# Order of the DMA transposes between two token blocks of a hybrid decoder block, with its low-rank products and router moved

## The chip, the core and the metric

The kernel runs on one core of a Trainium2 chip. The core has TensorE for matmuls, VectorE, ScalarE and GpSimd (POOL) for the rest, and SyncE, which here does nothing but hand DMAs to one queue in program order. All engines run at the same time and wait for each other through semaphores. The metric is the time of the device for one call, in microseconds (us), as the median of several runs.

## The reference

One decoder layer over 2048 tokens of width 1024. It computes a gated linear attention (GLA) and a multi-scale causal pooling from the same normed input, gates and merges the two, projects the result, and feeds it to a mixture of experts (32 experts in 4 groups, the best group and its two best experts for each token).

```python
h = rmsnorm(x, norm1_g)
q, k, v, r, a_low, u_pool, gate_gla, gate_pool = jnp.split(h @ w_in, split_idx, axis=-1)
log_a = jax.nn.log_sigmoid(a_low @ w_alpha_up + b_alpha) / 16.0      # a_low has 16 columns
o = gla_mix(q, k, v, log_a)
o = head_rmsnorm(o, gla_norm_g) * jax.nn.silu(r)
merged = jax.nn.sigmoid(gate_gla) * (o @ w_gla_branch) + jax.nn.sigmoid(gate_pool) * (pool_mix(u_pool, ...) @ w_pool_branch)
x = x + merged @ w_out
h2 = rmsnorm(x, norm2_g)
x = x + hier_moe(h2, w_router_group, ..., w_exp_gate, w_exp_up, w_exp_down)   # router: 36 logits per token
return rmsnorm(x, norm_f_g)
```

## The kernel before

The mixer, everything up to `h2` and the router, works through the tokens in four blocks of 512 (0 to 3), each as four tiles of 128 rows (t0 to t3). The experts follow when all blocks are done. Float32 values are split into a high and a low half of 16 bits, so a product of 128x128 by 128x512 is made of three matmuls ("passes"); in every block TensorE runs, one after another: `p3` (v and r, seven products of 24 matmuls each), `qk`, the GLA steps with the pooling's products between them, `gates(0)` and `merge(0)`, `gates(1)` and `merge(1)`, and the output product.

Operands with the contraction in the partitions come from transposes that the DMA engines make, issued on SyncE's queue (`TQ` is "sync"):

- `turned` (line 771) transposes one tile's half of GLA's or the merged rows. `merge(1)` makes four of them, one a tile, after `L845` on VectorE, `L847` on POOL, `L769` on ScalarE and `L770` on POOL. The output product `out_mm` (line 859) reads them as `mT[t][1]`; those of `merge(0)` are `mT[t][0]`.
- `p0_turn` (line 259) transposes the normed input of the next block: eight DMAs for tiles 0 and 2 (i = 0) and eight for tiles 1 and 3 (i = 1), of each eight four into `hT` and four into `hS` (sums of tiles, which `p3` and others use).
- `out_turn` (also line 259, `bt<-bt`) transposes the normed output rows `h2`, two DMAs a tile, for the router's logits (`logits`, line 881).

At the end of a block, `out_mm(t, 0)` and `out_mm(t, 1)` give the left and right half of tile t's output; the string `OUT` sets the order in which they and the work between them are written: `m0` and `n0` are the two halves of tile 0, `t0` is its `out_turn`, `b` is `p1b` and `c` is `p1c`. `p1a` (line 441) computes the 16 columns of `a_low` for the next block from all of `hT`: 24 narrow matmuls, four side by side, and one copy. `p1b` (line 453) expands them to 256 columns and takes the log-sigmoid and running sums on ScalarE (lines 458 to 463) and VectorE (466 to 468); `p1c` makes the decay factors. `out_norm` adds to x (line 862, VectorE), stores, and norms the row (lines 240, 242, 251).

A block's logits and its counting of tokens by expert (`route`, lines 1036 to 1128) are run inside the next block's `p3`: its list `fill` has one entry ahead of each product, `N2` empty ones, then the logits of t0 to t3; `route` follows `p3`.

What is written is not yet the order that runs. A scheduler with a cost model of its own orders each engine's instructions by what it expects to be ready; `issue_after(ins)` adds an edge, so that what is traced inside it and runs on the engine of `ins` stands behind `ins`. Each engine, SyncE's queue too, then runs its list strictly in order.

Where block b hands over to b + 1 is called boundary b here: the output product of b, with the transposes of b + 1, and the start of `p3` of b + 1. There are three, and block 0 differs in one point: the weights are loaded in float32 (line 159), split by ScalarE (175) and VectorE (176) and stored for later blocks (179), which load the halves (168).

Of the kernel before, what the change touches and what calls it, by code (L numbers as in the profile page):

```python
# [36 lines left out]
class Mixer:  # L37
# [727 lines left out]
    def turned(self, x, lo):  # L765

        nc = self.nc
        hl, o = self.bt([128, 2, 512], F16), self.bt([128, 8, 128], F16)
        nc.scalar.activation(hl[:, 0], x, AF.Copy)  # L769
        self.on(lo).tensor_tensor(hl[:, 1], x, hl[:, 0], op=OP.subtract)  # L770
        getattr(nc, self.TQ).dma_start(o, hl.rearrange("p a c -> p (a c)"), transpose=True)
        return o

    def pool_u(self, b, g):
# [47 lines left out]
        self.seven(self.L7, GG0 + 4 * c, GP0 + 4 * c, self.et, post, fill)  # L822
        return s

    N0, N1, N2, NK = 3, 0, 2, 3
    OUT = 'm0 m1 b m2 m3 w n0 c n1 t0 n2 t1 n3 t2 t3'
    LAST = 'm0 s0 m1 t0 s1 l0 f0 m2 t1 s3 l1 f1 n3 s4 l2 f3 r01 t3 l3 r23 f4'

    def merge(self, c, s, fill=()):
# [57 lines left out]
    def block(self, b, tail):  # L887

        last = b + 1 == self.NB
        self.blk = b  # L890
        self.hT, self.L7, self.L7c = self.hTn, self.sevens(self.Hn, self.HSn), self.sevens_c(self.Hn, self.HSn)
        self.kend = [None, None]
        self.oT, self.mixT, self.mT, self.xo = [], [None] * 4, [[] for _ in range(TT)], {}
        self.v, self.rs = {}, {}
        if b:
            self.p3([lambda: None] * self.N2 + tail[:4])
            tail[4]()
        else:
            self.p3([lambda: None] * 2 + [self.p1a, self.p1b, self.p1c])
        s0, s1 = self.qk(0), self.qk(1)  # L900
        for f in s0 + s1[:self.NK]:
            f()
        self.p2t(0)
        for f in s1[self.NK:]:
            f()
        self.p2t(1)
        steps = []
        for t in range(TT):
            g = self.gla_a(t)
            if t % 2 == 0:  # L910
                steps = self.pool_u(b, t)
            for f in steps[:4]:
                f()
            steps = steps[4:]
            self.gla_b(t, *g)
        sg = self.gates(0)
        self.merge(0, sg)
        nx, non = [], lambda: None
        steps = [] if last else self.p0_norm(b + 1, 0, nx)
        sg = self.gates(1, [non] * self.N0 + steps)  # L920
        if not last:
            self.p0_turn(0, nx, self.DM[1])
            nx = []
            steps = self.p0_norm(b + 1, 1, nx)
        self.merge(1, sg, [non] * self.N1 + steps)
        if not last:
            self.p0_turn(1, nx, self.DM[1])
            self.p1a()
        hh, h2 = {}, {}

        def turn(t):
            h2[t] = self.out_turn(hh[t], self.DM[2] and not (last and t >= self.DM[3]))

        def logits(t):
            self.logits(t, h2[t])

        def mm(t, hf, mid=None):
            self.out_mm(b, t, hf, wo, mid)
            if hf:
                hh[t] = self.out_norm(b, t, last and t >= self.QT)  # L940

        wo = {hf: [self.weight("wv", O0 + 4 * hf + j) for j in range(4)] for hf in range(2 if last else 1)}
        if last:
            nc = self.nc
            nc.vector.tensor_scalar(self.g2, self.g2, float(D) ** 0.5, None, op0=OP.mult)
            self.xo = {t: self.x_load(b, t) for t in range(TT)}
            mm(0, 0)
            self.early.close()
            self.mw = self.ctx.enter_context(self.tc.tile_pool(name="mw", bufs=1))
            s, n = self.weights(0), self.weights(1)  # L950
            for i in (0, 1, 3, 4):
                self.fetch(s, i)
            self.first = [s, n]

            def split(i):
                with self.tc.issue_after(self.done[-2]), self.tc.issue_after(self.done[-1]):
                    self.split1(s, i)

            def fetch(i):
                with self.tc.issue_after(self.turning):  # L960
                    self.fetch(n, i)

            acts = {"m": lambda t: (mm(t, 0), mm(t, 1)) if t else mm(t, 1), "t": turn, "l": logits,
                    "n": lambda t: (mm(t, 0), mm(t, 1, lambda: turn(t - 1))),
                    "s": split, "f": fetch}
            for c in self.LAST.split():
                if c[0] == "r":
                    self.route(b, int(c[1]), len(c) - 1)
                else:
                    acts[c[0]](int(c[1]))  # L970
            self.mid.close()
            self.mq = self.ctx.enter_context(self.tc.tile_pool(name="mq", bufs=1))
            self.gf = self.mq.tile([128, D], F32, name="gfr")
            self.nc.sync.dma_start(self.gf, self.A["gfr"].to_broadcast([128, D]))
            for i in (2, 5):
                self.fetch(s, i)
            return None
        def wo1():
            wo[1] = [self.weight("wv", O0 + 4 + j) for j in range(4)]

        acts = {"m": lambda t: mm(t, 0), "n": lambda t: mm(t, 1), "t": turn, "w": lambda t: wo1(), "b": lambda t: self.p1b(),
                "c": lambda t: self.p1c()}
        for c in self.OUT.split():
            acts[c[0]](int(c[1:] or 0))
        return [lambda t=t: logits(t) for t in range(TT)] + [lambda: self.route(b)]
# [673 lines left out]
```

## Time and profile before

| | us |
|---|---|
| median of 3 runs | 1665.48 |
| lowest, highest | 1657.59, 1665.78 |
| the profiled execution | 1663.56 |
| its span in the trace | 1661.7 |
| TensorE busy (matmuls) | 1517.5 |
| VectorE busy | 1064.5 |
| ScalarE busy | 650.6 |
| POOL busy | 519.9 |
| TensorE waiting for transposes of line 771 (L859) | 13.0 |
| TensorE waiting for transposes of line 259 into bt (L881) | 15.0 |
| mean granted clock of TensorE | 0.965 |

The boundaries lie at about 281 to 400 us (0), 545 to 660 (1) and 812 to 930 (2). An engine's idle time costs something only where TensorE, or what TensorE waits for, comes later by it.

### The profile page before, as it was taken

The page shows a single profiled execution, that of the slowest core. Times are in us where ns is not written, and L with a number is a line of the kernel's source. Part 1 is how long each engine was busy: PE and PEld are TensorE (multiplying, and loading weights), DVE is VectorE, ACT ScalarE, POOL GpSimd, SP SyncE. Part 2 cuts the span into 40 slices and gives each one's busy share as a digit, 9 for nine tenths or more (in the row PEclk, how much of TensorE's full clock was granted, in tenths as well). Part 3 has the DMA queues.
Part 4 walks back from the last instruction along what each step waited for, and adds up shares of the span by engine and source line. Part 5 has one row for each costly group of instructions (what it writes and reads, how often), then busy time and mean ns, then how long its engine had stood idle before and what let it go on. Part 6 is the DMA issues. An engine that isn't in the chain of part 4 may idle for free. (4 is left out here: it accounts for less than half of the span.)

```text
span 1661.7 us, 27589 instructions
## 1 busy us (share of the span) xinstructions
PE 1517.5 (91%) x10635; PEld 915.8 (55%) x10635; DVE 1064.5 (64%) x1941; ACT 650.6 (39%) x1023; POOL 519.9 (31%) x499
## 2 busy tenths in 40 slices
PE   4888997898999898999988999996799999999995
PEld 2365442345744344854433774443668687777873
DVE  8999796447744344772624774337577777777773
ACT  5633454431123241122323121123356665666651
POOL 1034243222414311432411341131333444444431
PEclk9899999999999999999999999998799999999998
DMA  8866678898466959566879755759599999999950
GB/s 289 253 226 213 215 258 186 275 367 247 153 194 198 255 167 293 173 198 179 212 198 255 235 169 177 215 155 313 193 320 331 333 329 341 334 328 327 321 190 36
DMA packets 247337, 400.96 MB, mean 241 GB/s; under 512 B 154731, under 2 KB 159211, under 8 KB 247200
## 3 DMA queue, kind: packets, MB, share of 16 engines
q1 hardware_dynamic: 224672, 330.79, 64.0%
q0 software_dynamic: 22528, 68.35, 11.6%
q8 instruction: 85, 1.39, 0.3%
q14 instruction: 52, 0.43, 0.1%
HBM read 300.33 MB, written 75.50 MB: 226 GB/s over the span
## 5 line engine op out<-in xcount | busy, mean ns | idle before, releaser
L1391 PE MATMUL acc<-xT,mwh 128*128 128x184 f16 (+2 forms) x3264 | 249.3, 238 | 0.0
L1391 PEld LDWEIGHTS <-mwh 128*128 128x128 f16 x3264 | 244.1, 98 | 7.7 <-issue 7.5
L859 PE MATMUL acc<-w,bt 128*128 128x512 f16 x768 | 173.1, 387 | 21.2 <-DMA bt<-bt 13.0
L842 PE MATMUL acc<-w,bt 128*128 128x512 f16 x768 | 170.0, 383 | 8.3 <-ACT w L175 8.3
L1297 DVE SCALAR_TENSOR_TENSOR mwh<-mst,mwh 128x1024 f16<-128x1024 f32 x128 | 153.4, 1219 | 24.0 <-ACT mwh L1296 24.0
L1296 ACT ACTIVATE mwh<-mst 128x1024 f16<-128x1024 f32 x128 | 128.8, 1049 | 54.1 <-PE acc L1391 53.3
L522 PEld LDWEIGHTS <-w 128*128 128x128 f16 x1344 | 129.5, 99 | 35.1 <-issue 11.6
L859 PEld LDWEIGHTS <-bt 128*128 128x128 f16 x768 | 75.7, 99 | 117.5 <-DMA bt<-bt 14.0
L842 PEld LDWEIGHTS <-bt 128*128 128x128 f16 x768 | 75.4, 98 | 101.5 <-issue 12.9
L339 PEld LDWEIGHTS <-hS 128*128 128x128 f16 x768 | 75.6, 98 | 95.0 <-issue 5.7
L175 ACT ACTIVATE w<-w 128x1024 f16<-128x1024 f32 x74 | 74.9, 1029 | 113.2 <-DVE w L398 33.5
L176 DVE SCALAR_TENSOR_TENSOR w<-w 128x1024 f16<-128x1024 f32 x74 | 98.3, 1342 | 29.9 <-ACT w L175 29.6
L1416 PE MATMUL acc<-msd,sg 128*128 128x512 f32 x256 | 115.7, 604 | 0.0
L847 POOL TENSOR_TENSOR et<-et 128x512 f32<-128x512 f32 x32 | 43.4, 1358 | 201.6 <-DVE et L845 201.6
L522 PE MATMUL acc<-hS,w 128*128 128x256 f16 x768 | 93.4, 274 | 4.7 <-DVE w L176 3.0
L339 PEld LDWEIGHTS <-hT 128*128 128x128 f16 x576 | 56.3, 98 | 71.4 <-issue 5.1
L769 ACT ACTIVATE bt<-et 128x512 f16<-128x512 f32 x48 | 30.1, 628 | 167.1 <-POOL et L847 105.6
L845 DVE SCALAR_TENSOR_TENSOR et<-acc,et 128x512 f32<-128x512 f32 x64 | 43.5, 689 | 80.4 <-PE acc L842 80.4
L339 PE MATMUL aux<-w,hS 128*128 128x512 f16 x384 | 89.7, 384 | 3.0 <-DVE et L757 2.6
L339 PE MATMUL acc<-w,hS 128*128 128x512 f16 x384 | 88.3, 379 | 0.0
L819 ACT ACTIVATE et<-et 128x512 f32<-128x512 f32 x64 | 39.6, 628 | 101.8 <-DVE et L348 101.7
L1416 PEld LDWEIGHTS acc<-msd,sg 128*128 128x128 f32 x256 | 47.8, 192 | 55.8 <-issue 46.7
(307 smaller groups left out, 2602.1 us busy)
## 6 DMA issues: line engine op xcount, KB each, us to landing
w<-wkeep SPq DMA_DIRECT2D x210, 512.0 KB, 4.6
mst<-in_we_dram SPq DMA_DIRECT2D x128, 512.0 KB, 6.2
wkeep<-w SPq DMA_DIRECT2D x70, 512.0 KB, 3.0
msd<-in_we_dram SPq DMA_DIRECT2D x64, 512.0 KB, 7.0
w<-in_wv_dram SPq DMA_DIRECT2D x40, 512.0 KB, 5.1
x<-in_x_dram SPq DMA_DIRECT2D x32, 512.0 KB, 5.4
out_dram<-x POOLq DMA_DIRECT2D x16, 512.0 KB, 7.1
h2d<-bt POOLq DMA_DIRECT2D x32, 256.0 KB, 6.8
```

The source lines that it names most:

```text
L175: nc.scalar.activation(w[:, 0, c:], f[:, c:], AF.Copy, scale=WSC)
L176: nc.vector.scalar_tensor_tensor(w[:, 1, c:], f[:, c:], WSC, w[:, 0, c:], op0=OP.mult, op1=OP.subtract)
L339: nc.tensor.matmul(p, L[name](i, c, k), w[k // 2][:, a, (k % 2) * 512:(k % 2 + 1) * 512], start=k == 0 and m == 0, stop=k == 3 and m == 2)
L522: nc.tensor.matmul(ps[:, :h], w[:, i, k * 128:(k + 1) * 128], L[name](c, k), start=k == 0 and m == 0, stop=k == 3 and m == 2)
L842: nc.tensor.matmul(ps, lhs, w[k // 2][:, a, (k % 2) * 512:(k % 2 + 1) * 512], start=k == 0 and i == 0, stop=k == 3 and i == 2)
L845: nc.vector.scalar_tensor_tensor(x, ps, DSC * ASC, x, op0=OP.mult, op1=OP.mult)
L847: self.on('madd').tensor_tensor(x, x, s[t, 1], op=OP.add)
L859: nc.tensor.matmul(ps, self.mT[t][k // 4][:, 4 * c + k % 4], w[hf][k // 2][:, a, (k % 2) * 512:(k % 2 + 1) * 512], start=k == 0 and i == 0 ...
L1296: nc.scalar.activation(w[:, 0], f, AF.Copy, scale=WSC)
L1297: nc.vector.scalar_tensor_tensor(w[:, 1], f, WSC, w[:, 0], op0=OP.mult, op1=OP.subtract)
L1391: nc.tensor.matmul(ps[:, c * CAP + lo:c * CAP + hi], self.part(W[o], col, 128, a), xT[:, b, k, lo:hi], start=k == 0 and i == 0, stop=k == ...
L1416: nc.tensor.matmul(ps, s["ac"][i][:, f, :128], self.part(s["W"][3 * i + 2], f * D + hf * 512, 512), start=f == 0, stop=f == 1)
```

## The change

The last transpose of each call of `turned` is remembered, and `p0_turn(1)` is traced behind it, so that SyncE has the four transposes of the merged rows ahead of those eight. `p1a` moves from ahead of the output tiles to behind the third one (`a`), `p1b` from behind the second to behind the fourth. `N2` grows from 2 to 3, so that each set of logits stands ahead of the product after the one before which it stood.

```diff
@@ turned
-        getattr(nc, self.TQ).dma_start(o, hl.rearrange("p a c -> p (a c)"), transpose=True)
+        self.turned1 = getattr(nc, self.TQ).dma_start(o, hl.rearrange("p a c -> p (a c)"), transpose=True).ins
@@
-    N0, N1, N2, NK = 3, 0, 2, 3
-    OUT = 'm0 m1 b m2 m3 w n0 c n1 t0 n2 t1 n3 t2 t3'
+    N0, N1, N2, NK = 3, 0, 3, 3
+    OUT = 'm0 m1 m2 a m3 b w n0 c n1 t0 n2 t1 n3 t2 t3'
@@ block
         if not last:
-            self.p0_turn(1, nx, self.DM[1])
-            self.p1a()
+            with self.tc.issue_after(self.turned1):
+                self.p0_turn(1, nx, self.DM[1])
@@
-        acts = {"m": lambda t: mm(t, 0), "n": lambda t: mm(t, 1), "t": turn, "w": lambda t: wo1(), "b": lambda t: self.p1b(),
+        acts = {"m": lambda t: mm(t, 0), "n": lambda t: mm(t, 1), "t": turn, "w": lambda t: wo1(), "a": lambda t: self.p1a(), "b": lambda t: self.p1b(),
```

What the scheduler makes of it on SyncE's queue at boundary 1, before (L771 are the merged rows, hT and hS the next block's input, w weights):

```order
L168 DMA w<-wkeep 128x2048 x3
L259 DMA_TRANSPOSE hT<-et 128x8x128 x8
L259 DMA_TRANSPOSE hS<-et 128x8x128 x4
L273 DMA x<-in_x_dram 128x1024 x2
L168 DMA w<-wkeep 128x2048 x3
L771 DMA_TRANSPOSE bt<-bt 128x8x128
L168 DMA w<-wkeep 128x2048
L771 DMA_TRANSPOSE bt<-bt 128x8x128
L168 DMA w<-wkeep 128x2048
L771 DMA_TRANSPOSE bt<-bt 128x8x128 x2
```

Here the merged rows come last. SyncE's queue at boundary 1 with the change:

```order
L168 DMA w<-wkeep 128x2048 x3
L259 DMA_TRANSPOSE hT<-et 128x8x128 x4
L168 DMA w<-wkeep 128x2048
L273 DMA x<-in_x_dram 128x1024 x2
L168 DMA w<-wkeep 128x2048 x2
L771 DMA_TRANSPOSE bt<-bt 128x8x128
L168 DMA w<-wkeep 128x2048
L771 DMA_TRANSPOSE bt<-bt 128x8x128
L168 DMA w<-wkeep 128x2048
L771 DMA_TRANSPOSE bt<-bt 128x8x128 x2
L259 DMA_TRANSPOSE hT<-et 128x8x128 x4
L259 DMA_TRANSPOSE hS<-et 128x8x128 x4
```

The four L771 now stand ahead of four hT and four hS, which were all of p0_turn(1); the first four hT, those of p0_turn(0), stay where they were, and five weight loads keep their places among the rest. Boundary 2 reads the same.

On SyncE's queue at boundary 0, before (w from in_wv are weights in float32, wkeep their stores):

```order
L159 DMA w<-in_wv_dram 128x1024
L259 DMA_TRANSPOSE hT<-et 128x8x128 x4
L159 DMA w<-in_wv_dram 128x1024
L259 DMA_TRANSPOSE hS<-et 128x8x128 x2
L179 DMA wkeep<-w 128x2048
L259 DMA_TRANSPOSE hS<-et 128x8x128 x2
L159 DMA w<-in_wv_dram 128x1024
L273 DMA x<-in_x_dram 128x1024
L179 DMA wkeep<-w 128x2048
L273 DMA x<-in_x_dram 128x1024 x3
L159 DMA w<-in_wv_dram 128x1024
L179 DMA wkeep<-w 128x2048
```

Here the transposes stand between the first weights. SyncE's queue at boundary 0 with the change:

```order
L159 DMA w<-in_wv_dram 128x1024
L273 DMA x<-in_x_dram 128x1024 x2
L159 DMA w<-in_wv_dram 128x1024
L273 DMA x<-in_x_dram 128x1024 x2
L179 DMA wkeep<-w 128x2048
L159 DMA w<-in_wv_dram 128x1024
L179 DMA wkeep<-w 128x2048
L159 DMA w<-in_wv_dram 128x1024
L179 DMA wkeep<-w 128x2048
L159 DMA w<-in_wv_dram 128x1024
L179 DMA wkeep<-w 128x2048
L159 DMA w<-in_wv_dram 128x1024
```

All eight transposes of p0_turn(1) have left this stretch, and six weight loads stand where four stood; the transposes follow behind the four L771, eight rows later.

On VectorE at boundary 1, before (L862 adds an output tile to x, L466 to L468 are p1b):

```order
L862 SCALAR_TENSOR_TENSOR x<-acc,x 128x512 x2
L466 TENSOR_SCALAR bt<-aux,cst 128x512 x2
L467 TENSOR_TENSOR bt<-bt 128x512
L468 SCALAR_TENSOR_TENSOR bt<-rmask,bt 128x512
L467 TENSOR_TENSOR bt<-bt 128x512
L468 SCALAR_TENSOR_TENSOR bt<-rmask,bt 128x512
L862 SCALAR_TENSOR_TENSOR x<-acc,x 128x512 x3
```

Here two of the four sums stand behind p1b's chain. VectorE at boundary 1 with the change:

```order
L862 SCALAR_TENSOR_TENSOR x<-acc,x 128x512 x4
L466 TENSOR_SCALAR bt<-aux,cst 128x512 x2
L467 TENSOR_TENSOR bt<-bt 128x512
L468 SCALAR_TENSOR_TENSOR bt<-rmask,bt 128x512
L467 TENSOR_TENSOR bt<-bt 128x512
L468 SCALAR_TENSOR_TENSOR bt<-rmask,bt 128x512
L862 SCALAR_TENSOR_TENSOR x<-acc,x 128x512
```

The sums of all four left halves (m0 to m3) now stand ahead of p1b's chain, and behind it comes the sum of n0 alone. On TensorE at boundaries 1 and 2 the narrow products L441 stood ahead of the first output tile and stand now behind 72 matmuls of it; the scheduler now completes each tile's 24 matmuls before the next, where it had 29 that need no merged row of `merge(1)` ahead of the first that does.

## Rows read from the trace of the kernel before

**Rows 1.** The page, its head: span and number of instructions
```profile
span 1661.7 us, 27589 instructions
```

**Rows 2.** Waits of TensorE, whole span: line <- releaser, total us, times, longest
```profile
PE aux L881 <- DMA bt<-bt: 15.0, 10, 3.9
...
PE acc L859 <- DMA bt<-bt: 13.0, 2, 6.7
```

**Rows 3.** TensorE in order of time, boundary 1: start, us, what, count, idle before
```profile
544.46 20.88 PE L842 MATMUL acc<-w,bt 128*128 128x512 f16 x96
...
566.68 6.43 PE L859 MATMUL acc<-w,bt 128*128 128x512 f16 x29
...
579.86 7.23 PE L859 MATMUL acc<-w,bt 128*128 128x512 f16 x24 [6.74 <-DMA bt<-bt]
...
588.64 30.16 PE L859 MATMUL acc<-w,bt 128*128 128x512 f16 x139
...
634.48 4.63 PE L638 MATMUL aux<-w,hS 128*128 128x512 f16 x12
...
643.34 0.19 PE L881 MATMUL aux<-wrh,bt 128*128 128x36 f16 x1 [0.56 <-DMA bt<-bt]
```

**Rows 4.** TensorE, boundary 2 in time, then the router's waits at boundaries 0, 1, 2
```profile
847.05 6.76 PE L859 MATMUL acc<-w,bt 128*128 128x512 f16 x24 [6.29 <-DMA bt<-bt]
...
PE aux L881 <- DMA bt<-bt: 3.5, 4, 2.1
...
PE aux L881 <- DMA bt<-bt: 5.0, 3, 3.9
...
PE aux L881 <- DMA bt<-bt: 6.4, 3, 3.2
```

**Rows 5.** SyncE's DMA queue in order of time, boundary 1: start, us of issuing
```profile
547.20 15.09 SPq L259 DMA_TRANSPOSE hT<-et  x8
...
571.64 3.02 SPq L771 DMA_TRANSPOSE bt<-bt  x1
...
616.67 6.91 SPq L259 DMA_TRANSPOSE bt<-bt  x2
...
628.26 12.31 SPq L259 DMA_TRANSPOSE bt<-bt  x2
```

**Rows 6.** POOL in order of time, boundary 1, the merged rows' lower halves
```profile
560.38 1.16 POOL L770 TENSOR_TENSOR bt<-et,bt 128x512 f16<-128x512 f32 x1 [0.74 <-ACT bt L769]
...
567.38 2.28 POOL L770 TENSOR_TENSOR bt<-et,bt 128x512 f16<-128x512 f32 x2
```

**Rows 7.** Line 771 over the whole span, from issue to landing
```profile
DMA to landing us min/median/max: 3.0/3.3/8.2
```

**Rows 8.** Stretches at boundary 1: us, busy by engine, PEclk, DMA share, GB/s
```profile
545.00:566.00 21.00, 21.00 (x111) 9.39 (x112) 8.79 (x12) 4.57 (x7) 11.12 (x9) 1.00 1.02 255
...
619.00:640.00 21.00, 16.58 (x89) 7.33 (x87) 7.85 (x11) 5.51 (x7) 4.32 (x8) 0.84 1.17 258
```

**Rows 9.** Boundary 0 in order of time, TensorE, then SyncE's queue
```profile
281.20 3.57 PE L842 MATMUL acc<-w,bt 128*128 128x512 f16 x8 [6.56 <-ACT w L175]
...
327.51 22.58 PE L859 MATMUL acc<-w,bt 128*128 128x512 f16 x96 [4.45 <-DVE x L862]
...
275.55 7.18 SPq L259 DMA_TRANSPOSE hT<-et  x4
...
291.58 0.58 SPq L159 DMA_DIRECT2D w<-in_wv_dram  x1
```

**Rows 10.** VectorE in order of time, boundary 1: end of p1b's chain, first normed row
```profile
597.78 1.22 DVE L468 TENSOR_TENSOR_SCAN bt<-rmask,bt 128x512 f32<-128x512 bf16 x1
...
609.77 1.23 DVE L251 TENSOR_TENSOR bt<-x,bt 128x1024 f16<-128x1024 f32 x1 [0.52 <-ACT bt L251]
```

**Rows 11.** VectorE in order of time after boundary 1: last logits, input of the counting
```profile
657.57 0.18 DVE L883 SCALAR_TENSOR_TENSOR L<-aux,brow 128x36 f32<-128x36 f32 x1
...
667.45 0.28 DVE L1062 TENSOR_TENSOR rt32b<-rt,rt 128x128 bf16<-128x128 f32 x1
```

## The prediction

> **What bounds the kernel now.** The profiled execution took 1663.56 us, 1.9 us more than its span [rows 1]; the median of the three runs is 1665.48 us. I make the sum against 1663.56. TensorE is the engine to watch: in the three places where one block of tokens hands over to the next, the view of waits shows what it stood still for. Two rows concern transposes made by the DMA queue: 13.0 us in two waits ahead of the output product, L859, and 15.0 us in ten waits ahead of the router's products, L881 [rows 2]. The chain that ended last is no help here; it consists of tiny pieces.
>
> Then I read TensorE in order of time at the handover from block 1 to block 2 (boundary 1). The merge's 96 matmuls end at 565.3, the narrow products (p1a) take 1.4, and after 29 output matmuls TensorE waits 6.74 us. The 24 matmuls behind the wait take 7.23 us, while 139 later ones take 30.16, or 0.217 each; between the two, p1b takes 1.6 [rows 3]. Twenty-four at that pace are 5.2, so slow matmuls after the wait cost another 2.0, and this wait costs 8.8. At boundary 2 it is 6.29 + (6.76 - 5.2) = 7.8 [rows 4]. The router's waits are 3.5, 5.0 and 6.4 at boundaries 0, 1 and 2 [rows 4], and 12 matmuls after them take 4.63 instead of 2.6 [rows 3]: 16.9 in all.
>
> Why the merged rows are late: POOL finishes the first of the four (t0) at 561.5 and the last (t3) at 569.7 [rows 6], but SyncE's queue hands t0 over only at 571.64 [rows 5], behind eight hT and four hS transposes; TensorE resumes at 579.86, 8.2 later.
>
> **What the change does, part by part.** *Boundary 1.* The same instructions run, in another order. SyncE now has the four merged transposes ahead of p0_turn(1)'s eight. t0 can be handed over at 561.5 instead of 571.64. TensorE wants it after twelve matmuls, at 565.3 + 2.6 = 567.9. With the landing seen here, 8.2, it lands at 569.7, a wait of 1.8; with the median landing of this line, 3.3 [rows 7], there is none. I take 1, since five loads still stand ahead of it. t1 to t3 are wanted 5.2 apart and are ready 3 apart; they are covered.
>
> The displaced hT transposes come next, and the narrow products of p1a want all of them. Eight took 15.09, 1.89 each [rows 5]. From 569.7 the fourth starts at 575.4 and lands 3.3 to 8.2 later, 578.7 to 583.6. p1a now stands behind three output tiles, 72 matmuls: 565.3 + 15.6 = 580.9. Wait: 0 to 2.7, I take 1. The far bound is the price of a transpose in a full queue, 3.02 for t0 and 12.31 for the two of L259 at 628.26 [rows 5]; with 3.7 each and the long landing the wait is 8.1. hS is wanted a whole output phase later, and the four weight loads behind it are not needed before the next block: nothing. So boundary 1 keeps 2 of 8.8 and boundary 2 keeps 2 of 7.8: **12.6 gained**, with bounds of -1 and 16.6.
>
> The Trainium skill (Advanced Engine Details and Errata, X-Bar Transpose) says that transposing DMAs run as fast as plain ones, at 350 to 400 GB/s. As an estimate by that page the 262 KB of one would take 0.7 us; no wait at p1a would be left and the sum would be 2 us better. Here one took 1.89 in a row of eight, so the trace decides.
>
> *p1b.* It moves with p1a to behind the fourth tile, and its chain over ScalarE and VectorE stands in VectorE's order ahead of the sum of n0 (L862). At boundary 1 that chain ended at 599.0 [rows 10], 11.9 after TensorE reached p1b (579.86 + 7.23). Now p1b comes at 565.3 + 97 x 0.217 + 1.4 + 2 = 589.7, so n0's sum waits until 601.6, though its matmuls are done by about 597. TensorE is not held up: n0 to n3 have four accumulators and the next block wants the first one after about 22 us of matmuls. ScalarE's and VectorE's work is covered by the 41.7 us of output matmuls. If that cover fails, the price is the wait for VectorE seen in block 0, within the 13.7 below.
>
> *Router one product later.* One product is 24 matmuls, 5.2 us. The next block starts now at 565.3 + 41.7 + 1.4 + 1.6 + 2 = 612.0, before at 618.8, and the normed rows are ready about 1.7 earlier (601.6 against 603.3 for n0's sum). Relative to the block they are 5 later, which nearly eats the 5.2. But the first pair of transposes had slack: its data were ready at 611.0 [rows 10] and it was handed over at 616.67 [rows 5], behind weight loads that wait for TensorE and so move with it. I therefore let the landings keep their distance to the block start. t0's wait then goes. t1 landed at 643.3 [rows 3], 24.5 after the start, and is now wanted after four products and one set of logits, 21.4: about 3 remain. Boundary 1 gains 4 of 7, boundary 2 about 2.5, boundary 0 about 2: **8.5**. Bounds: 0 and all 16.9. The counting after the router gets less cover: from the last logits to the sums that TensorE reads took 657.57 to 667.7 [rows 11], 10.2, and the order now leaves 24 matmuls at 0.217 and 43 of half the width at half of it, 9.9. That is 0.3 to 1 per boundary: **-2**.
>
> *Boundary 0.* Here the weights are being split, and SyncE loads them between the transposes: the four hT took 7.18, and the output weights' first load went out only at 291.58 [rows 9]. From 281.20 to 350.0 TensorE has 240 matmuls (52.1), p1a 1.4 and p1b 1.6; 13.7 are lost. Of that, 8 slow matmuls at 281.20 (3.57 for 1.7) follow a load whose place doesn't change. The other 11.8 are waits for weights and one of 4.45 for VectorE, which sat in p1b's chain [rows 9]. In the new order the four output weights leave before any of p0_turn(1)'s transposes, with only their own stores between; that is 8 us or more earlier, and p1b's chain comes when all four sums are done. I take **9**, bounds 4 and 11.8.
>
> Sum: 12.6 + 8.5 - 2 + 9 = 28. 1663.6 - 28 = **1636 us**.
>
> **The rivals.** *The wait is handed on.* For it: the DMA engines are full while these transposes run, a share of 1.02 from 545 to 566 and 1.17 from 619 to 640 [rows 8]; an order does not make work smaller. Then hT lands late in the full queue, 4 or 5 of the 8 come back at p1a, the router's rows land at the old absolute time and the boundaries gain some 3 each, block 0 some 4: gain 7 to 13, about **1653**. Against it: merged rows are wanted at once, hT three tiles later. The skill (DMA: Bandwidth & Descriptors, Issuing engines are not separate DMA queues) has all queues interleave on the same 16 engines, which speaks for this rival; the share over 1 agrees.
>
> *Slower: the narrow products become the plug.* p1a is in TensorE's order, so the rest of the output waits with it. If the displaced hT cost 3.7 us or more each, p1a waits 8 at every boundary; slow matmuls behind it add 2, and p1b, the norms and so the router's rows come 8 later, which adds 3 to the router's waits. It decides from about 9 us of wait at p1a, where it exceeds what was removed. Per boundary -2 to -5, against block 0's weights at +3: about **1673**. Against it: t0 to t3 are handed over spread out, so less is queued.
>
> *Everything goes.* All 16.6, 16.9 and 11.8: up to 45 less, about **1620**.
>
> *It doesn't do what it says.* The built order shows the four transposes ahead in all three boundaries, so I give this next to nothing.
>
> **How the numbers follow.** Forecast 0.62 (1630 to 1648), handed on 0.22, everything 0.08, slower 0.08. For 8 in 10 the range runs from 1622 to 1657. More than 0.5% (8.3 us, about what a measurement of this kernel can tell from no change) faster: the forecast, the upper case and some 0.09 of the second, 0.79. Within: 0.13. Slower: 0.08.
>
> **What would show it.** Right: no wait over 2 us ahead of L859 at boundaries 1 and 2, L441 behind 72 matmuls with at most 2.7 of wait, L881's total down to about 7, the next block of block 0 starting near 341. Wrong: a wait of over 5 at L441; L881's total unchanged; new waits for VectorE at L859 or L638; waits at L1065 over 1 us in the three boundaries; or block 0 still short of weights.

## The result, and the profile after

The changed kernel takes 1647.65 us in the median of six runs (1646.32 to 1648.67), the kernel before 1664.76 in six (1657.59 to 1666.55): a ratio of 0.9898, 95% interval 0.9882 to 0.9915, some 17 us. That is faster by more than 0.5% and inside the range of 1622 to 1657. The forecast itself, 1636, is 12 us too low, and that is what the experiments had to explain. Executions of one kernel differ: on one chip the kernel before ran between 1659.78 and 1670.87 us.

The head of the page of the changed kernel; the profiled execution took 1646.32 us, against 1663.56 before [rows 1]:

```profile
span 1644.5 us, 27592 instructions
```

TensorE's waits over the whole span (line <- releaser, total us, times, longest), answering to [rows 2]:

```profile
PE aux L881 <- DMA bt<-bt: 18.3, 7, 4.7
...
PE aux L1065 <- DVE rt32b L1062: 9.9, 3, 4.9
...
PE acc L859 <- DMA bt<-bt: 1.9, 1, 1.9
...
PE aux L441 <- DMA hT<-et: 0.4, 1, 0.4
```

The output product's 13.0 us are nearly gone and the narrow products (L441) hardly wait. But the router's wait, 15.0 before, is now 18.3.

TensorE at boundary 1 in order of time (start, us, what, count, idle before), answering to [rows 3]:

```profile
563.31 15.70 PE L859 MATMUL acc<-w,bt 128*128 128x512 f16 x72
578.94 0.39 PE L441 MATMUL aux<-hT,wah 128*32 128x512 f16 x1
...
608.40 2.75 PE L638 MATMUL aux<-w,hT 128*128 128x512 f16 x12
...
630.91 0.19 PE L881 MATMUL aux<-wrh,bt 128*128 128x36 f16 x1 [1.02 <-DMA bt<-bt]
...
633.80 0.22 PE L881 MATMUL aux<-wrh,bt 128*128 128x36 f16 x2 [2.67 <-DMA bt<-bt]
...
634.36 4.44 PE L638 MATMUL aux<-w,hS 128*128 128x512 f16 x12
...
652.79 1.47 PE L522 MATMUL acc<-hT,w 128*128 128x256 f16 x12
```

72 output matmuls run without a gap, then the narrow products without a wait. The second tile's logits stand still for 1.02 and 2.67 us, and the 12 matmuls behind them take 4.44 in place of 2.75.

Boundary 0 on TensorE, the same columns:

```profile
342.31 2.75 PE L638 MATMUL aux<-w,hT 128*128 128x512 f16 x12
...
371.03 0.19 PE L881 MATMUL aux<-wrh,bt 128*128 128x36 f16 x1 [2.66 <-DMA bt<-bt]
...
380.62 0.21 PE L881 MATMUL aux<-wrh,bt 128*128 128x36 f16 x1 [4.72 <-DMA bt<-bt]
...
380.70 5.22 PE L638 MATMUL aux<-w,hS 128*128 128x512 f16 x12
...
408.65 0.22 PE L1065 MATMUL aux<-rt32b,tri 128*128 128x128 bf16 x1 [2.04 <-DVE rt32b L1062]
```

In the kernel before, `p3` of block 1 began at 349.93, and its first logits, after a wait of 0.19 us, at this time:

```profile
371.00 0.19 PE L881 MATMUL aux<-wrh,bt 128*128 128x36 f16 x1 [0.19 <-DMA bt<-bt]
```

The block starts 7.6 us sooner and the first logits come at 371.03 instead of 371.00. At this boundary the router's rows did not move with the block.

### The profile page after: what moved, and what is told of

Same layout as the page of the kernel before. It is cut to its first block, busy times and chain, and to the rows that moved or that the text cites. A ratio compares the mean times of both kernels' runs of the same rounds, so it can differ in the third digit from the quotient of the medians.

```text
span 1644.5 us, 27592 instructions
## 1 busy us (share of the span) xinstructions
PE 1516.8 (92%) x10635; PEld 916.5 (56%) x10635; DVE 1063.8 (65%) x1941; ACT 648.3 (39%) x1021; POOL 523.8 (32%) x499
## 5 line engine op out<-in xcount | busy, mean ns | idle before, releaser
L842 PE MATMUL acc<-w,bt 128*128 128x512 f16 x768 | 169.4, 382 | 9.2 <-ACT w L175 9.2
L859 PE MATMUL acc<-w,bt 128*128 128x512 f16 x768 | 168.8, 379 | 3.5 <-DMA bt<-bt 1.9
L522 PEld LDWEIGHTS <-w 128*128 128x128 f16 x1344 | 131.0, 99 | 33.7 <-issue 9.3
L859 PEld LDWEIGHTS <-bt 128*128 128x128 f16 x768 | 74.4, 98 | 95.6 <-issue 5.8
L522 PE MATMUL acc<-hS,w 128*128 128x256 f16 x768 | 95.1, 277 | 4.5 <-DVE w L176 3.0
```

Source lines behind the costliest of these rows:

```text
L522: nc.tensor.matmul(ps[:, :h], w[:, i, k * 128:(k + 1) * 128], L[name](c, k), start=k == 0 and m == 0, stop=k == 3 and m == 2)
L842: nc.tensor.matmul(ps, lhs, w[k // 2][:, a, (k % 2) * 512:(k % 2 + 1) * 512], start=k == 0 and i == 0, stop=k == 3 and i == 2)
L859: nc.tensor.matmul(ps, self.mT[t][k // 4][:, 4 * c + k % 4], w[hf][k // 2][:, a, (k % 2) * 512:(k % 2 + 1) * 512], start=k == 0 and i == 0 ...
```

## The experiments

All ratios are to the kernel before on the same chip; the kernels ran on several chips. I read the traces for where time goes, and the ratios for how much; a difference between two kernels is that of their ratios, in us of a run of 1665. The letter names in the texts on record: **F**, the router's rows land at a time of their own; **P**, the prediction's working; **Q**, the loads of x in SyncE's queue hold the transposes back; **S**, the norms are late because they wait for a store; **D**, the DMA engines have too much to move at that time; **0**, no effect.

| kernel | median, us | ratio, 95% interval |
|---|---|---|
| the change | 1647.65 | 0.9898 (0.9882 to 0.9915) |
| E1: without the router's step | 1653.04 | 0.9929 (0.9905 to 0.9952) |
| E2: the router's step alone | 1658.35 | 0.9948 (0.9927 to 0.9968) |
| E5: the queue's order alone | 1657.46 | 0.9940 (0.9923 to 0.9957) |
| E6: without the queue's order | 1667.24 | 0.9986 (0.9969 to 1.0002) |
| E3: the change, loads of x later | 1633.52 | 0.9810 (0.9774 to 0.9845) |
| E7: before, loads of x later | 1658.63 | 0.9951 (0.9931 to 0.9970) |
| E11: E3 without the router's step | 1648.83 | 0.9881 (0.9859 to 0.9903) |
| E9: the change, loads of x on GpSimd's queue | 1667.47 | 1.0001 (0.9984 to 1.0018) |
| E12: E3 with loads that nobody reads | 1645.22 | 0.9881 (0.9861 to 0.9900) |
| E4: the change, norm to its own tile | 1647.13 | 0.9893 (0.9852 to 0.9934) |
| E8: E3 and E4 together | 1644.70 | 0.9866 (0.9847 to 0.9885) |
| E10: E3, norm to its own tile in block 0 | 1636.60 | 0.9807 (0.9786 to 0.9828) |

### The parts of the change

**E1**, the change without its third part:

```diff
-    N0, N1, N2, NK = 3, 0, 3, 3
+    N0, N1, N2, NK = 3, 0, 2, 3
```

> The changed kernel with the router's products one step sooner again (N2 = 2): the third part of the change undone alone. Theory F (landings fixed in time): the rows of the router's second token tile land when the DMA queue lets them, whenever TensorE starts the block; then a product fewer ahead of the waiting logits is a product more behind them, 5.2 us (two groups of 12 matmuls of 2.6) at each of the three boundaries, less what the clock gives back: 1655 to 1663 us. Theory P (the prediction's working): the shift is worth 8.5 us, so about 1656 us with all of it as longer L881 waits (18.3 us now, about 27 then). Theory 0 (the shift does nothing, the wait only moves): 1646 to 1649 us.

0.9929: some 5 us slower than the change, though the two intervals just overlap (0.9905 and 0.9915). F asked for 1655 to 1663, P for 1656, "0" for at most 1649; 1653 lies between them, and speaks against "0" only by times. The profiled execution, at 1647.39 the fastest of six, did not show the loss, so the trace cannot say where the others have it.

**E2**, the third part alone, N2 = 3 in the kernel before.

> The kernel before with only the router's products one step later (N2 = 3); order of the transposes and narrow products as before. Theory F: the landings do not move, so each boundary gains up to one product of 5.2 us: 1650 to 1657 us. Theory P: the 8.5 us of the prediction less the loss on the clock, about 1657 to 1659 us. Theory 0: 1662 to 1667 us. If the two parts add up, this gain and the gain of the other two parts (E1 against before) together make the 17 us of the whole change.

0.9948, 8.7 us: the 8.5 that the prediction gave to this step, within P and just above F's upper end. TensorE's wait at L881 fell from 15.0 to 8.9 us, and L859's stayed:

```profile
PE acc L859 <- DMA bt<-bt: 12.6, 2, 7.0
...
PE aux L881 <- DMA bt<-bt: 8.9, 5, 3.4
```

So a product later is worth what the prediction said as long as the block does not start earlier. The gains do not add up: 8.7 for this step and 11.8 for the other two parts (E1) would make 20.5, and the whole change has 17.0.

**E5**, the first part alone: `issue_after(self.turned1)` around `p0_turn(1)`, with `p1a` still written directly behind it, OUT and N2 as before.

> The kernel before with the first part of the change alone: the four transposes of the merged rows go ahead of the next block's eight on SyncE's queue; the narrow products stay ahead of the first output tile and the router's products stay where they were. Theory 'the parts need each other': the output tile's wait (L859, 13.0 us in 2) goes, but the narrow products (L441), first in the phase, now wait for the last hT transpose instead; with the whole change that was issued at 574.7 us, 11.4 us after its output phase began at 563.3, so with 2 to 3 us to land a wait of about 13 us at each of boundaries 1 and 2, 26 us in place of 13: 1672 to 1680 us, slower than before. Theory 'each part pays alone': the output waits go and L441 finds its rows, 1651 to 1655 us.

0.9940, 10 us faster; my first theory falls, and the second just misses (1657.46 against 1651 to 1655). TensorE at boundary 1 of E5, in order of time:

```profile
564.66 15.27 PE L859 MATMUL acc<-w,bt 128*128 128x512 f16 x70
579.86 0.39 PE L441 MATMUL aux<-hT,wah 128*32 128x512 f16 x1
```

The narrow products are written ahead of the first output tile and run behind 70 output matmuls, without a wait: the scheduler saw that their rows come later and moved them by itself. At this place the second part of the change writes down what the first brings about. From the start of `merge(1)` to `p3` E5 takes 65.81 us at boundaries 1 and 2 each (before 74.18 and 73.58, the change 65.81 and 67.93), and block 1 starts at 343.13 (before 349.93, the change 342.31), so this one part carries nearly the whole gain of the output phases; E1, which has the second part too, cannot be told from E5.

**E6**, the change without that first part (no `issue_after`).

> The changed kernel without its first part: the narrow products behind an output tile and the router's products one step later, the queue's order as before. Theory 'the parts need each other': the first output product stands where the narrow ones stood, 5 to 8 us sooner, and waits so much longer for the merged rows at boundaries 1 and 2 (6.7 and 6.3 us before, 8 to 12 then); the gain of boundary 0 in the output phase (7.8 us) and of the router's step (about 5) stay: 1653 to 1662 us. Theory 'each part pays alone': 1665 less the 6 to 10 of these two parts and no new wait, 1655 us or under, with L859's waits on the merged rows at 13 us as before. The trace decides by these waits.

0.9986, not to be told from no change. TensorE at boundary 1:

```profile
563.25 7.93 PE L859 MATMUL acc<-w,bt 128*128 128x512 f16 x36
577.86 10.13 PE L859 MATMUL acc<-w,bt 128*128 128x512 f16 x36 [6.68 <-DMA bt<-bt]
```

The merged rows are waited for as before, 6.68 us, not the 8 to 12 that I expected: 36 matmuls now run ahead of the wait instead of 29. By the ratios E6 is another 6 us behind E2, which differs from it by the moved narrow products, though in the profiled executions E6 is 2 us ahead of E2 where the experts begin. This stays open. The queue's order is the part without which the change gives nothing that can be measured.

### Why the router's wait grew

SyncE's queue of the changed kernel at boundary 1 (start, us of issuing), answering to [rows 5]; line 273 loads x for block 3:

```profile
605.93 0.33 SPq L273 DMA_DIRECT2D x<-in_x_dram  x1
...
608.17 7.59 SPq L259 DMA_TRANSPOSE bt<-bt  x2
...
617.39 0.58 SPq L273 DMA_DIRECT2D x<-in_x_dram  x1
...
618.54 11.11 SPq L259 DMA_TRANSPOSE bt<-bt  x2
```

Such a load waits for the norm that frees its buffer, and then goes out just ahead of the transposes of that norm's rows. VectorE's first norm that reads one of these rows runs at 778, over 170 us later.

**E3** puts these loads behind the last of the router's transposes:

```diff
+            self.rturned = self.turning      # in turn(t), after out_turn
...
-                xs.append(self.x_load(b, t))
+                with self.tc.issue_after(self.rturned):
+                    xs.append(self.x_load(b, t))
```

(for blocks 2 and 3, and likewise around the last block's `x_load`).

> The changed kernel with one thing more: the loads of x for a later block, which stand on SyncE's queue between the transposes of the router's rows and wait there for the norm of the tile whose buffer they reuse, are put behind the last of these transposes (boundaries 0, 1 and 2). Nothing is left out. Theory Q (the order on SyncE's queue holds the router's transposes back): the second pair goes out some 4 to 5 us sooner at boundaries 0 and 1 (now 371.5 and 618.5 us, the rows are ready at about 613.5 at boundary 1), L881's waits fall from 18.3 to under 10 us, time 1636 to 1642 us. Theory S (the norms are late, because they wait for the store of the rows they overwrite): the pairs of tiles 2 and 3 stay where they are, under 3 us in all, 1644 to 1648 us. Theory D (the DMA engines are full, the order does not matter): the transposes go out sooner and land as late as now, 1645 to 1649 us.

0.981: 1633.52, another 15 us by the ratios (14 by the medians), the best of all with E10, and below even Q's 1636 to 1642. S and D, as I had put them, fall. L881's total is 8.5 us. SyncE's queue of E3 at boundary 1:

```profile
607.04 4.83 SPq L259 DMA_TRANSPOSE bt<-bt  x2
...
614.73 10.35 SPq L259 DMA_TRANSPOSE bt<-bt  x2
...
637.88 2.47 SPq L273 DMA_DIRECT2D x<-in_x_dram  x4
```

Both kernels start the first pair 0.23 us ahead of `p3`; it takes 4.83 us to issue in place of 7.59, so the second starts 7.5 after the block's start instead of 10.1. The stretch of `p3`, `608.40:652.79` after and `607.27:647.40` in E3 (us, busy PE, PEld, DVE, ACT, POOL, granted clock, DMA share, GB/s), one row from each kernel:

```profile
608.40:652.79 44.39, 40.70 (x265) 19.19 (x264) 23.90 (x49) 12.46 (x21) 9.62 (x14) 0.96 1.08 328
```

```profile
607.27:647.40 40.13, 39.17 (x265) 18.89 (x264) 23.93 (x49) 12.46 (x21) 9.61 (x14) 1.00 1.07 305
```

4.3 us shorter, and the granted clock, 0.96 after, is 1.00. In both the DMA engines are full (1.08 and 1.07). Boundary 2 has the larger part: there the first pair takes 4.57 us to issue instead of 9.96, and `p3` with the router 41.00 instead of 48.37. At boundary 0 the first pair takes 10.83 instead of 10.01, and the block behind reaches `gates(0)` only 1.1 us sooner (448.22 and 449.35).

Two explanations fit: the loads stand in the way in the queue (Q), or their bytes do (D: 44.39 us at 328 GB/s are 14.6 MB, 40.13 at 305 are 12.2). **E9** has the same loads at nearly the same place in time, on another queue (`nc.gpsimd.dma_start` instead of `nc.sync.dma_start`, the edges of E3 taken out).

> The changed kernel with the same loads of x as in E3 neither later nor fewer, but on GpSimd's queue, each behind the store of the tile whose buffer it reuses; SyncE's queue then has only weights between the router's transposes. It tells the queue's order from the load on the DMA engines. Theory Q (the loads stood ahead of the transposes in the one queue): most of E3's 14 us is kept, 1632 to 1638 us, and the second pair of transposes at boundary 1 is issued near 614.7 as in E3, not 618.5. Theory D (what matters is that 2 MB less are moved while the transposes run): the pairs are issued sooner but land as late as now, and the stores of the rows take as long, 1643 to 1649 us.

1.0001, 17 us behind the change: all that it had gained is lost, and TensorE waits longer for the router's rows than in any other kernel:

```profile
PE aux L881 <- DMA bt<-bt: 26.4, 7, 8.8
```

SyncE's queue of E9 at boundary 1, where `p3` starts at 620.86:

```profile
620.62 7.02 SPq L259 DMA_TRANSPOSE bt<-bt  x2
...
630.32 14.34 SPq L259 DMA_TRANSPOSE bt<-bt  x2
```

No load of x is left in this queue, and yet the first pair takes 7.02, near the 7.59 with the loads and far from 4.83. Q, as I had put it, falls. So does D: it expected "as now". Most of the loss lies elsewhere, at boundary 0. SyncE's queue there in the changed kernel, with the loads between the transposes (rows between left out):

```profile
359.30 10.01 SPq L259 DMA_TRANSPOSE bt<-bt  x2
...
371.48 7.86 SPq L259 DMA_TRANSPOSE bt<-bt  x2
...
380.07 6.11 SPq L259 DMA_TRANSPOSE bt<-bt  x4
```

In E9 at boundary 0, SyncE's queue, then TensorE:

```profile
357.17 15.04 SPq L259 DMA_TRANSPOSE bt<-bt  x2
...
374.06 19.68 SPq L259 DMA_TRANSPOSE bt<-bt  x6
...
389.85 0.21 PE L881 MATMUL aux<-wrh,bt 128*128 128x36 f16 x1 [8.76 <-DMA bt<-bt]
```

The eight transposes take 34.7 us to issue instead of 24.0, and the block behind reaches `gates(0)` at 461.81 instead of 449.35, 12.5 later; `p3` with the router of boundary 1 takes only 1.4 more, that of boundary 2 no more. The store does not explain it: VectorE's first norm of boundary 0 waits for it as long as after (5.54 and 5.66 us). At boundary 1, where that wait is longer (10.9 us against 8.2 after), little is lost. Why the loads hurt more from the other queue stays open. The Trainium skill (DMA: Bandwidth & Descriptors, Issuing engines are not separate DMA queues) says that DMAs from all issuing engines interleave on the same 16 DMA engines; E9 agrees, since loads on GpSimd's queue lengthen the transposes on SyncE's from 24.0 to 34.7 us.

**E12** puts bytes back into E3 that wait for no norm: two loads of 512 KB into a tile that nobody reads, behind the first and behind the second pair, and a third behind the last.

> E3 with loads that nobody reads, into a tile of their own: 512 KB (rows of x) behind the router's transposes of the first tile and again behind those of the second at boundaries 0, 1 and 2, so that about 1 MB is moved again between the pairs, and a third behind the last pair. They wait for no norm and no buffer that the kernel uses. Theory D (the transfers of the block's first products fill the DMA engines, and the router's rows land when the sum of the bytes lets them; 12.2 MB in 40.1 us in E3, 14.6 MB in 44.4 us in the changed kernel at boundary 1): 1 MB more costs 1 MB over about 300 GB/s, 3.3 us at each boundary, 6 to 10 us in all, 1639 to 1645 us. Theory Q (the loads of x hurt by waiting in the queue for a norm's buffer, not by their bytes): 1632 to 1636 us as E3.

0.9881: 11.8 us lost against E3, a little more than D's 6 to 10; Q said none. The trace gives D less than the times do. SyncE's queue of E12 at boundary 1, `p3` from 609.96:

```profile
609.72 4.81 SPq L259 DMA_TRANSPOSE bt<-bt  x2
614.59 1.37 SPq L942 DMA_DIRECT2D xd<-in_x_dram  x1
...
619.36 9.14 SPq L259 DMA_TRANSPOSE bt<-bt  x2
```

With the load behind it, the first pair takes 4.81 as in E3; the second goes out 9.4 after the block's start instead of 7.5. But in this execution, at 1640.14 the fastest of four, boundaries 1 and 2 then lost nothing (`p3` of block 2 took 40.2 us, 40.1 in E3), boundary 0 lost 2.7, and some 5 lie in the experts' stage, by the chip (last section). So loads that wait for no norm cost time in the median, but where is not seen, and they stand in the queue as well as in the DMA engines, so their place and their bytes are not told apart.

What the first pair takes to issue, in us (after and E9 have a load of x ahead of it, E3 and E12 have not):

| | after | E3 | E9 | E12 |
|---|---|---|---|---|
| boundary 0 | 10.01 | 10.83 | 15.04 | 11.15 |
| boundary 1 | 7.59 | 4.83 | 7.02 | 4.81 |
| boundary 2 | 9.96 | 4.57 | 6.01 | 5.01 |

At boundaries 1 and 2 the pair is slower behind such a load, in either queue. At boundary 0 it is slow without one too, and E12's second pair of boundary 1, with a load ahead of it, takes 9.14 against 10.35 in E3. That each boundary pays by its bytes is not shown.

**E7**, the edit of E3 in the kernel before.

> The kernel before with only the loads of x for a later block put behind the last router's transpose (the edit of E3, which gave 14 us on top of the change). Theory Q1 (the loads in the queue held the router's rows back in both kernels): L881's waits fall from 15.0 us to under 7 and the time to 1652 to 1658 us. Theory Q2 (it is the change that brought the queue to the point where the loads hold it up: before, the norms came late enough): under 4 us, 1661 to 1667 us.

0.9951, 8 us, between Q1 and Q2. L881's wait falls from 15.0 to 9.0, L859's 12.7 stays. The loads cost time in both kernels, and more in the changed one (15 us).

**E11**, E3 with N2 = 2.

> E3 with the router's products one step sooner again (N2 = 2). In the changed kernel that step was worth about 5 us (E1). Theory F (it is worth what the rows come late): in E3 the second tile's logits at boundary 1 start at 628.6 without a wait over 1 us, a product sooner they would stand near 623 and wait about 3 us there, as much at boundary 2, and boundary 0 by up to 5.2 more: 1637 to 1645 us. Theory 0 (with the loads out of the way the rows come early enough): 1632 to 1636 us.

0.9881: the step that is worth about 5 us in the change is worth 12 here, more than F asked for (1648.83 against 1637 to 1645). TensorE at boundary 1 of E11:

```profile
630.20 0.19 PE L885 MATMUL aux<-wrh,bt 128*128 128x36 f16 x1 [4.14 <-DMA bt<-bt]
```

The second tile's logits wait for 4.14 us, where E3 waits for 0.22 at 629.02. F's mechanism holds: the block of E11 starts 2.5 us after that of E3 (609.76 and 607.27), the rows are there at 630.2 and 629.0, and the one product more ahead of them in E3 covers it.

### The store under the norm

**E4** lets L242 write to a tile `y` of its own, so that it need not wait until the row is stored:

```diff
-        nc.vector.scalar_tensor_tensor(x, x, r[:, 0:1], g, op0=OP.mult, op1=OP.mult)
+        y = x if store is None else self.x2.tile([128, D], F32, name="y", bufs=1)
+        nc.vector.scalar_tensor_tensor(y, x, r[:, 0:1], g, op0=OP.mult, op1=OP.mult)
+        x = y
```

> The changed kernel with the output norm writing to a tile of its own (L242 no longer in place), so that it does not wait for the store of the rows (out_dram from x). Nothing is left out. Theory S: VectorE's waits for that store (25.8 us in 7 now) go, the rows of tiles 2 and 3 are ready up to 5 us sooner, time 1640 to 1645 us with L881's waits at 10 us or less. Theory Q: the rows then wait in SyncE's queue, no change, 1646 to 1649 us. Theory D: the waits on the store go and the landings stay, 1645 to 1649 us.

0.9893, no change: S falls. VectorE waited 25.8 us for these stores in the changed kernel, and taking that away gave nothing: the rows then wait for the transposes (L881's total is 20.4 us, 18.3 after). **E8** adds it to E3, **E10** to E3 in block 0 alone.

> E3 and E4 together: the loads of x behind the router's transposes, and the output norm writing to a tile of its own, so that it does not wait for the store of its rows. Theory S (with the queue free, the norms are what is late): at boundary 0 VectorE waits 5.6 us for the store ahead of the first tile's norm in E3, and its logits wait 2.8 and 2.8 us; both go, and half of L881's other 3 us: 1625 to 1630 us. Theory 'nothing left there': L881's waits of E3 (8.5 us in 7) come from the transposes' own time in the queue and stay, 1631 to 1635 us.

> E3 with the output norm of block 0 alone writing to a tile of its own. In E8 this was done in all blocks: boundary 0 gained 4 us on E3 (the next block's L848 at 444.35 after 448.22), boundaries 1 and 2 lost 3 and 5. Theory 'the wait for the store hurts only where it comes first, at boundary 0': 1627 to 1631 us. Theory 'E8 lost by the tile itself' (its buffer, the norms' instructions in another order): 1634 to 1645 us.

E8 is 0.9866, slower than E3 and outside both theories: boundary 0 gained 4 us, boundaries 1 and 2 lost 3 and 5 to new router's waits (the longest 5.5); the first tile's norm ran sooner there (at boundary 2 852.33 after 855.07), the second tile's did not (862.82 after 862.62). E10 keeps boundary 0's side of it. VectorE's first norm of boundary 0, in E3 and in E10:

```profile
350.52 1.28 DVE L242 SCALAR_TENSOR_TENSOR x<-x,rms,g2r 128x1024 f32<-128x1024 f32 x1 [5.60 <-DMA out_dram<-x]
```

```profile
344.34 1.28 DVE L243 SCALAR_TENSOR_TENSOR y<-x,rms,g2r 128x1024 f32<-128x1024 f32 x1 [0.94 <-POOL rms L210]
```

The norm comes 6 us sooner, the products `qk` of the last block begin at 900.15 instead of 902.26, and the time, 0.9807, cannot be told from E3's 0.981. I expected 1627 to 1631 or over 1634; 1636.60, on a chip where the kernel before took 1667.00 and not 1665.49, decides nothing.

## Why the prediction was right, point by point

The balance, from the traces. An output phase is read from the start of block 1's or 2's `merge(1)` (boundary 0: from a point ahead of it that moved by 0.16 us) to the first matmul of `p3`; the router's part from there to the first L522 of the next block (boundary 0: to the next `merge(1)`).

| | output phase, predicted | measured | router, predicted | measured |
|---|---|---|---|---|
| boundary 0 | 9 | 7.8 | 2 | -5.8 |
| boundary 1 | 6.8 | 8.4 | 4 | 1.8 |
| boundary 2 | 5.8 | 5.65 | 2.5 | -2.75 |
| counting | | | -2 | within the above |
| sum | 21.6 | 21.85 | 6.5 | -6.75 |

The spans differ by 17.2: 15.1 of this table and 2.1 behind boundary 2, which I had not forecast.

- **Merged rows, 12.6 predicted: 14.05 measured.** The mechanism and the size hold. One wait of 1.94 us stays at boundary 2, under the 2 that was granted. The narrow products wait for 0.4 us in all instead of 1 each; the displaced transposes were quicker than assumed: eight in a row had taken 15.09 us before [rows 5], the eight of `p0_turn(1)` now took 10.9 (570.61 to 581.49). E5 and E6 show that the queue's order carries this part. That the narrow products must be moved by hand for it, as E5's first theory had it, was wrong: the scheduler moves them.
- **Boundary 0, 9 predicted: 7.8.** The next block starts at 342.31, near the 341 named. Of the 11.8 that the prediction calls waits, the trace of before has 8.2 as waits, 3.8 for weights and 4.4 for VectorE; the rest are slow matmuls and gaps.
- **p1b: nothing predicted, nothing seen** on TensorE; there is no wait for VectorE at L859 any more.
- **The router's products, 8.5 predicted, 6.5 with the counting: -6.75, the step that failed.** The step is "I therefore let the landings keep their distance to the block start". The prediction had worked out that the normed rows come only 1.7 us sooner while the block starts some 7 sooner, and then overruled it. E2 shows that the shift alone is worth the 8.5 (8.7 measured), E1 that on top of the other parts it gives about 5: not the shift was mis-sized, but what the earlier start costs the rows.
  - At boundary 0 the step failed. The first tile's pair was handed over at 359.30 instead of 360.84 and took 10.01 us to issue instead of 9.02; its rows landed 28.7 us after the block's start instead of 21.1. L881's wait rose from 3.5 to 7.4, and the granted clock from `p3` to `qk` fell from 1.00 to 0.88.
  - At boundary 1 it held: the second tile's first rows landed 24.7 us after the block's start before (643.34) and 22.5 after (630.91). The 4 became 1.8 because 3.7 us of wait stayed instead of about 3, and because the 12 matmuls behind it were slow again, 4.44 instead of 2.75; the prediction had priced that in the wait that goes and not in the one that stays.
  - At boundary 2 it failed by 3 to 4 us: the second tile's rows landed 26.1 and 29.1 us after the block's start instead of 23.0 and 25.3. Block start and second tile's logits, before and after:

```profile
885.36 2.75 PE L638 MATMUL aux<-w,hT 128*128 128x512 f16 x12
...
908.34 0.19 PE L881 MATMUL aux<-wrh,bt 128*128 128x36 f16 x1 [2.18 <-DMA bt<-bt]
...
910.65 0.22 PE L881 MATMUL aux<-wrh,bt 128*128 128x36 f16 x2 [1.01 <-DMA bt<-bt]
```

```profile
867.62 2.75 PE L638 MATMUL aux<-w,hT 128*128 128x512 f16 x12
...
893.72 0.19 PE L881 MATMUL aux<-wrh,bt 128*128 128x36 f16 x1 [2.41 <-DMA bt<-bt]
...
896.75 0.24 PE L881 MATMUL aux<-wrh,bt 128*128 128x36 f16 x2 [2.81 <-DMA bt<-bt]
```

- **The rival "the wait is handed on" had part of it.** It named the wrong receiver (the narrow products, which wait for 0.4 us) and a right one ("the router's rows land at the old absolute time"), which came true at boundary 0 alone. Its ground, the share of 1.17 [rows 8], belongs to boundary 1, where the rows moved with the block. E3 shows that loads which nobody needs yet have a large part in the lateness; whether by their bytes or by their place stays open.
- **The counting, -2: not seen.** L1065's total rose by 1.8 us, by one wait of 2.04 at boundary 0, and not by 0.3 to 1 at each boundary; two other waits of the counting (L1069, and L1122 for `Ak`) fell from 3.5 to 1.1 together.
- **"Slower" and "everything goes"** did not come; the wait at L441 that decides the first is 0.4.

The range held because it reached to 1657 for the rival in which part of the gain is handed back; the mis-sized term, from +6.5 to -6.75, is 13 us of just that. That 1647.65 still lies in the band of 1630 to 1648, which had 0.62, is in part luck: the 2.1 us behind boundary 2, which no term had, brought it there.

## What to carry to other kernels

When a wait is removed ahead of a stretch in which the DMA engines are already full, do not assume that the landings inside that stretch move along with its start (here they did at one boundary of three): work each one out from its own queue and from the bytes around it, and take the later of the two. Look through the queue for loads that are only there because a buffer came free; here moving them was worth 15 us on top of the change's 17, by edges that only set an order. And before a wait of an engine is priced, see what waits next on the same rows: 25.8 us of VectorE's waiting for stores were worth nothing.

## What the runs showed of the hardware that was not expected

Moving four loads a boundary to GpSimd's queue cost 17 us (ratios 1.0001 and 0.9898), more than leaving them in the crowded one; beside them the eight transposes of boundary 0 took 34.7 us to issue against 24.0.

The DMA engines were as busy with transposes at less than half the rate. Two stretches of the changed kernel, the first with nothing issued but the hT and hS transposes, the second mostly with loads and stores (columns as above, the last two are DMA share and GB/s):

```profile
572.00:582.00 10.00, 10.00 (x63) 4.14 (x62) 1.38 (x2) 0.41 (x1) 0.00 (x0) 1.00 1.03 182
```

```profile
342.00:362.00 20.00, 20.00 (x95) 9.06 (x93) 11.44 (x19) 10.60 (x17) 4.53 (x9) 1.00 1.03 418
```

The experts' stage, in which all these kernels do the same, ran in 451.8 to 453.7 us on the chip of E1 to E4 and in 456.5 to 458.5 on those of E5 to E12: one profiled execution of each, some 5 us that go with the chip and not with the kernel, which is why spans of different chips are not compared here without the ratios. The kernel before as a whole differed less between these chips (1665.49 on the first, 1668.80 and 1667.00 on the others). First and last start of its matmuls in E3 and E10 (duration in ns; first and last start in us):

```profile
L1397 PE MATMUL acc<-xT,mwh x3264: 187/243/314, 1149.1 to 1600.9; 128*128 128x184 f16 x169, 128*128 128x128 f16 x12, 128*128 128x56 f16 x11
```

```profile
L1399 PE MATMUL acc<-xT,mwh x3264: 187/243/314, 1147.8 to 1606.3; 128*128 128x184 f16 x169, 128*128 128x128 f16 x12, 128*128 128x56 f16 x11
```
